# A row gradient on one core: the third load of each group in two transfers, and the first store tied to the first of them

## The chip, the core and the metric

The kernel runs on one core of one Trainium2 chip. The time is device microseconds of one execution. Before the change the median of three runs is 1246.87 us (1246.65 to 1247.15). Next to these stands one profiled execution, whose records are the views shown here; it has a time of its own.

## The reference

```python
def setup_inputs():
    return {"x": np.random.randn(8192, 8192).astype(np.float32)}

def reference(x):
    return np.gradient(x, axis=1)
```

Along each row, an inner element of the result is half the difference of its two neighbours, `(x[j+1] - x[j-1]) / 2`. The two ends of a row are plain differences, `x[1] - x[0]` and `x[8191] - x[8190]`. 268.4 MB are read and as many written.

## The kernel before

The 8192 rows are cut into 32 tiles of 256 rows. Each of the 128 partitions holds two consecutive rows of the input side by side, so a tile is 128 x 16,384 float32, 8.39 MB, and one partition of it is 65,536 contiguous bytes of memory. Three slots in SBUF hold a tile each (`NB = 3`); tile `i` uses slot `i % 3`. A slot has 64 spare columns at its front (`SH = 64`): the input is loaded to columns 64 and up, the result is written in place from column 0, and is stored from there.

For each tile the program issues

- a load (line 52, `load`), on the queue of SyncE (SP), as all transfers;
- on GpSimd (POOL), line 74: the four end differences of the two rows of a partition, into a small tile `ends`; it waits for the load;
- on VectorE (DVE), line 80: one custom instruction over the whole tile that writes half the difference of the neighbours; it waits for line 74;
- line 91: a copy of the four end values to their places, on DVE for 20 tiles and on POOL for 12; it waits for line 80;
- a store (line 56, `store`); it waits for line 91.

The order is written out by hand (`manual_schedule`), so the order of the calls is the order on each engine. `chain` states for an instruction what it needs, and the waits follow from this.

Tiles are worked on in groups of three. The three loads of a group are issued one after another at the end of the group before (lines 103 to 106), each once the store of the tile that had the slot has landed. SP then comes to the group's stores. The first one, of the tile with `i % 3 == 0`, is issued as soon as its tile is finished. The second is held back (`held`, line 100) and carries an extra dependency on line 74 of the third tile (line 94, `at[0]`), that is, on the landing of the third load. The third follows when its tile is finished. All transfers run on the same 16 DMA engines in the order of issue, so reading and writing alternate: three loads, three stores, three loads.

The end differs a little. 32 tiles are ten groups and two tiles. In the last whole group (tiles 27, 28, 29) the loads of tiles 30 and 31 are issued right behind the store of tile 28 (lines 96 to 98), ahead of the store of tile 29; the stores of 30 and 31 end the program.

Of the kernel before, what the change touches and what calls it, by code (L numbers as in the profile page):

```python
# [1 line left out]

# [4 lines left out]


@with_exitstack
def kernel(  # L10
    ctx: ExitStack,
    tc: tile.TileContext,
    x: bass.AP,
    out: bass.AP,
):

    nc = tc.nc
    P = nc.NUM_PARTITIONS
    n, m = x.shape
    R = 2  # L20
    NB = 3
    SH = 64
    W = R * m
    nsets = n // (P * R)
    f32 = x.dtype

    x_sets = x.rearrange("(s p t) m -> s p (t m)", p=P, t=R)
    out_sets = out.rearrange("(s p t) m -> s p (t m)", p=P, t=R)

    pool = ctx.enter_context(tc.tile_pool(name="pool", bufs=1))  # L30
    edge = 256 // 4
    nends = nsets * R * 2
    ends_pad = pool.tile([P, nends + edge // 2], f32, name="ends", tag="ends")
    ends = ends_pad[:, 0:nends].rearrange("p (s t e) -> p s t e", t=R, e=2)
    slots = [pool.tile([P, SH + W], f32, name=f"slot{k}", tag=f"slot{k}") for k in range(NB)]
    loads, stores = [], [None] * nsets
    in_front = {}

    def chain(i, ins, *needed):

        group, engine = f"slot{i % NB}", ins.ins.engine
        keep = [o.ins for o in needed]
        if in_front.get(engine, (None,))[0] == group:
            keep.append(in_front[engine][1])
        tc.declare_no_dep(ins.ins, group=group, keep=keep, reason="implied by the needed step")
        tc.add_to_no_dep_group(group, ins.ins)
        in_front[engine] = group, ins.ins
        return ins

    def load(i):  # L50
        b = slots[i % NB]
        ins = nc.sync.dma_start(out=b[:, SH : SH + W], in_=x_sets[i])  # L52
        loads.append(chain(i, ins, *([stores[i - NB]] if i >= NB else [])))

    def store(i, done, later):
        ins = nc.sync.dma_start(out=out_sets[i], in_=slots[i % NB][:, 0:W])
        stores[i] = chain(i, ins, done)
        if later is not None:
            tc.add_manual_dep(
                ins.ins,  # L60
                later.ins.name,
                mybir.DependencyInfo(mybir.DependencyClass.Sync, mybir.DependencyReason.DATA),
                reason="issued once the next tile has landed",
            )

    held = None
    with tc.manual_schedule():
        for i in range(NB):
            load(i)
        for i in range(nsets):  # L70
            b = slots[i % NB]
            xin = b[:, SH : SH + W].rearrange("p (t m) -> p t m", m=m)

            ins = nc.gpsimd.tensor_sub(  # L74
                out=ends[:, i, :, :],
                in0=xin[:, :, 1 : m : m - 2],
                in1=xin[:, :, 0 : m - 1 : m - 2],
            )
            at = [chain(i, ins, loads[i])]
            ins = nc.vector._custom_dve(  # L80
                dve_ops.TENSOR_TENSOR_REDUCE_SUB_MAX,
                out=b[:, 1 : W - 1],
                in0=b[:, SH + 2 : SH + W],
                in1=b[:, SH : SH + W - 2],
                s0=0.0,
                s1=0.5,
            )
            halved = chain(i, ins, *at)
            res = b[:, 0:W].rearrange("p (t m) -> p t m", m=m)
            placer = nc.gpsimd if i % 5 in (1, 3) and i < nsets - 2 else nc.vector  # L90
            ins = placer.tensor_copy(out=res[:, :, 0 : m : m - 1], in_=ends[:, i, :, :])  # L91
            placed = chain(i, ins, halved)
            if held is not None:
                store(*held, at[0])
                held = None
                if i + 1 + NB > nsets - 1 and i % NB == NB - 1:
                    for k in range(i + 1, nsets):
                        load(k)
            if i % NB == 1 and i + 1 < nsets:
                held = i, placed  # L100
            else:
                store(i, placed, None)
            if i % NB == NB - 1:
                for k in range(i + 1, min(i + 1 + NB, nsets)):
                    if k >= len(loads):
                        load(k)


# [1 line left out]
_INS = ['x']  # L110
_OUTS = [((8192, 8192), 'float32')]


# [23 lines left out]
```

## Time and profile before

| what | value |
|---|---|
| median of three runs | 1246.87 us |
| profiled execution, its own time | 1247.28 us |
| span of its instructions | 1245.4 us |
| moved over the span | 536.88 MB, 431 GB/s |
| DVE busy | 554.6 us (45%) in 52 instructions |
| POOL busy | 8.9 us (1%) in 48 instructions |
| line 80, one instruction | 17.2 us |
| loads, issue to landing (median) | 57.9 us |
| stores, issue to landing (median) | 40.2 us |
| SP, one transfer's issue (median), load and store | 0.339 and 0.343 us |

The page cuts the span into 40 slices; a digit is the busy share of a slice in tenths, and the row GB/s says what the DMA engines moved in it. A group of instructions is shown as line, engine, operation, output<-input, shapes and count, then busy time and mean ns of one, then the idle time of the engine just before them and what ended it. Timeline rows are start, duration (both us), engine, line and operation; a number with x at the end of such a row counts the instructions that are merged in it. SPq is SP's sequencer, which issues the transfers. The transfer records give start, duration and size of every packet on the DMA engines.

### The profile page before, as it was taken

Reading aid. Unit: us, or ns where it says so; the run is one execution under the profiler, and the core shown is the slowest. Engines: PE = TensorE matmul, PEld = TensorE weight load, DVE = VectorE, ACT = ScalarE, POOL = GpSimd, SP = SyncE. Lnnn points to the kernel's source line nnn. Section 1 sums busy time; section 2 is a strip of 40 time slices with the busy share of each in tenths; the row PEclk is TensorE's granted clock in tenths of the full one; section 3 lists DMA queues with packets and bytes.
Section 4 is the critical chain, followed back from the end, with each engine's and each line's share of the span. In section 5 each row is a group of like instructions: output and inputs, shape, how many; then the busy total and the mean of one; then the engine's idle time right before and its main releaser. Section 6 shows DMA issues by size and latency. Waiting matters only on the chain.

```text
span 1245.4 us, 237 instructions
## 1 busy us (share of the span) xinstructions
DVE 554.6 (45%) x52; POOL 8.9 (1%) x48
## 2 busy tenths in 40 slices
DVE  2850483069009702850583079009603840591460
POOL 0000000000000000000000000000000000000000
DMA  9999999999999999999999999999999999999998
GB/s 404 436 432 415 436 438 438 438 438 436 434 427 425 432 438 438 436 425 436 429 432 436 438 438 429 436 432 438 432 429 434 438 432 438 438 429 436 432 432 370
DMA packets 9217, 536.88 MB, mean 431 GB/s; under 512 B 1024, under 2 KB 1024, under 8 KB 1024
## 3 DMA queue, kind: packets, MB, share of 16 engines
q1 hardware_dynamic: 9216, 536.88, 99.7%
q14 instruction: 1, 0.01, 0.0%
HBM read 268.44 MB, written 268.44 MB: 431 GB/s over the span
## 4 chain that ended last, share of the span: by engine, by line
another core or an unknown queue 67%; DVE 18%; DMA 10%; issue 2%; POOL 1%; SPq 0%; POOLq 0%
DVE slot L80 18%; DMA slot<-in_x_dram 6%; DMA out_dram<-slot 3%; POOL ends L74 0%; POOL slot L91 0%; SPq L52 0%; DVE slot L91 0%; POOLq L132 0%
## 5 line engine op out<-in xcount | busy, mean ns | idle before, releaser
L80 DVE CUSTOM_DVE_ANT_0 slot<-slot 128x16382 f32<-128x16382 f32 x32 | 551.2, 17224 | 649.0 <-POOL ends L74 649.0
L74 POOL TENSOR_TENSOR ends<-slot 128x4 f32<-128x4 f32 x32 | 6.4, 200 | 969.9 <-DMA slot<-in_x_dram 969.9
L91 POOL COPY slot<-ends 128x4 f32<-128x4 f32 x12 | 2.3, 192 | 207.9 <-DVE slot L80 207.9
L91 DVE COPY slot<-ends 128x4 f32<-128x4 f32 x20 | 3.4, 172 | 0.7
L121 POOL MEMSET const-bfloat16-1.0<- 128x1 bf16 x1 | 0.1, 102 | 0.0
L121 POOL MEMSET const-uint8-127<- 128x1 uint8 x1 | 0.1, 102 | 0.0
L121 POOL MEMSET const-float32-0.0<- 128x1 f32 x1 | 0.1, 99 | 0.2 <-issue 0.2
L121 POOL MEMSET const-float32-1.0<- 128x1 f32 x1 | 0.1, 99 | 0.0
## 6 DMA issues: line engine op xcount, KB each, us to landing
slot<-in_x_dram SPq DMA_DIRECT2D x32, 57.9
out_dram<-slot SPq DMA_DIRECT2D x32, 40.2
```

The source lines that it names most:

```text
L74: ins = nc.gpsimd.tensor_sub(out=ends[:, i, :, :], in0=xin[:, :, 1 : m : m - 2], in1=xin[:, :, 0 : m - 1 : m - 2],)
L80: ins = nc.vector._custom_dve(dve_ops.TENSOR_TENSOR_REDUCE_SUB_MAX, out=b[:, 1 : W - 1], in0=b[:, SH + 2 : SH + W], in1=b[:, SH : SH + W - 2],
L91: ins = placer.tensor_copy(out=res[:, :, 0 : m : m - 1], in_=ends[:, i, :, :])
L121: nc = _bacc.Bacc("TRN2", target_bir_lowering=False, num_devices=1)
```

## The change

The third load of each group, and the load of the last tile, is issued as two transfers: the first 15,104 columns, then the last 1,280 (`LAST`). Both wait for the same earlier store. `loads[i]` becomes a list of parts, and line 74 of the tile waits for all of them. The group's first store gets an extra dependency on the first part of the group's third load; in the two-tile end, the store of tile 29 gets one on the first part of the load of tile 31. The held second store keeps its dependency on line 74 of the third tile, the third store has none, as before. The instructions on POOL and DVE and their order are the same. SP has 75 transfers in place of 64: 11 loads are split, those of tiles 2, 5, ... 29 and of tile 31, and the order of the stores and the loads among each other stays.

```diff
+    LAST = 1280
@@
     def load(i):
         b = slots[i % NB]
-        ins = nc.sync.dma_start(out=b[:, SH : SH + W], in_=x_sets[i])
-        loads.append(chain(i, ins, *([stores[i - NB]] if i >= NB else [])))
+        freed = [stores[i - NB]] if i >= NB else []
+        cuts = [0, W - LAST, W] if i % NB == NB - 1 or i == nsets - 1 else [0, W]
+        parts = []
+        for lo, hi in zip(cuts, cuts[1:]):
+            ins = nc.sync.dma_start(out=b[:, SH + lo : SH + hi], in_=x_sets[i][:, lo:hi])
+            parts.append(chain(i, ins, *freed))
+        loads.append(parts)
@@
-                reason="issued once the next tile has landed",
+                reason="issued once this load has landed",
@@
-            at = [chain(i, ins, loads[i])]
+            at = [chain(i, ins, *loads[i])]
@@
             if i % NB == 1 and i + 1 < nsets:
                 held = i, placed
             else:
-                store(i, placed, None)
+                turn = loads[-1][0] if i % NB == 0 or i == nsets - NB else None
+                store(i, placed, turn if len(loads[-1]) > 1 else None)
```

## The prediction

> **What bounds the kernel now.** I read four views in this order: the page's slices of the span, the groups of instructions, the timeline around two ends of a group, and the transfer records in short stretches. The page comes first:
>
> ```profile
> DVE  2850483069009702850583079009603840591460
> DMA  9999999999999999999999999999999999999998
> GB/s 404 436 432 415 436 438 438 438 438 436 434 427 425 432 438 438 436 425 436 429 432 436 438 438 429 436 432 438 432 429 434 438 432 438 438 429 436 432 432 370
> ...
> L80 DVE CUSTOM_DVE_ANT_0 slot<-slot 128x16382 f32<-128x16382 f32 x32 | 551.2, 17224 | 649.0 <-POOL ends L74 649.0
> L74 POOL TENSOR_TENSOR ends<-slot 128x4 f32<-128x4 f32 x32 | 6.4, 200 | 969.9 <-DMA slot<-in_x_dram 969.9
> ```
>
> The 16 DMA engines are full in every slice; VectorE works 45% and always ends up waiting for a load. So only what the DMA engines lose can be won. Best slices move 438 GB/s, many 425 to 432. Where is the difference? In the timeline a POOL instruction of line 74 begins about 0.4 us after its load's last packet, so these rows are the loads' landings. Two ends of a group:
>
> ```profile
> 42.27 17.22 DVE L80 CUSTOM_DVE_ANT_0 slot<-slot 128x16382 f32<-128x16382 f32 x1 [1.85 <-POOL ends L74]
> ...
> 62.74 0.20 POOL L74 TENSOR_TENSOR ends<-slot 128x4 f32<-128x4 f32 x1 [2.99 <-DMA slot<-in_x_dram]
> 62.97 17.80 SPq L56 DMA_DIRECT2D out_dram<-slot  x2
> ```
>
> ```profile
> 390.28 40.12 SPq L56 DMA_DIRECT2D out_dram<-slot  x3
> 391.97 0.20 POOL L74 TENSOR_TENSOR ends<-slot 128x4 f32<-128x4 f32 x1 [19.17 <-DMA slot<-in_x_dram]
> ...
> 412.33 0.20 POOL L74 TENSOR_TENSOR ends<-slot 128x4 f32<-128x4 f32 x1 [20.16 <-DMA slot<-in_x_dram]
> ```
>
> The third load of the group landed 62.74 - 42.04 = 20.70 us after the second in the one (42.04 is the POOL row just ahead of the first line shown), 412.33 - 391.97 = 20.36 us in the other; other loads that follow a load come 19.1 to 19.3 us after it. The loss sits where a group's loads give way to its stores. A short stretch of the transfer records shows it (40 slices of 0.25 us; a packet is booked where it starts):
>
> ```profile
> GB/s 0 0 2359 1311 524 0 0 0 0 0 0 262 2884 524 524 0 0 0 0 0 0 0 0 0 0 0 262 2884 786 262 0 0 0 0 0 0 786 2621 524 262
> ```
>
> This is 55 to 65 us. Each DMA engine carries one row of 65,536 B at a time, 2.418 us each, so bursts of 16 starts should stand 2.4 us apart. They stand at 55.6, 58.1, then only at 61.8: the last packet of the third load took 1.2 to 1.4 us too long on all 16 engines, just ahead of the first store. I chained all packet records engine by engine. Almost every lengthened packet is the last one of a third load (a few are the first of the next loads); stores stay at 2.42 but for two or three. The amounts per engine are 1.2 to 1.4 us at the first switch, 0.3 to 1.05 at the fourth (412 us), 0 to 0.7 at the others. Over the run the engine that ends last collected 5.05 us of this, the four luckiest about 1.85 each. So 1.85 us falls on all engines together and 3.2 us is the lag of one engine behind the others: first landings and last landings of a transfer stand 0.6 us apart at the beginning and 3.5 us at the end.
>
> A check from the landings alone: the first loads of the groups come at 22.76 and, nine groups later, 1070.70, so a group takes 116.44 us, the quietest 115.87; 9 x 0.57 = 5.1 us. That is the whole prize.
>
> **The change, part by part.**
>
> *The wait.* The group's first store (line 56) was issued at 390.28, some 20 us before the engines could reach it; at 40.45 and 157.83 likewise. Now it waits for the first part of the third load, so SP holds it until then. Behind it on SP stand the group's second store, which already waited for the third load (issued at 62.97, 0.23 us after the landing), the third store, and the next loads, which wait for stores; none could go earlier than this point, and the second store is needed only 19.3 us after the first has begun. So nobody else becomes late. VectorE and POOL wait for both parts, which is the old landing. At the tail, the store of tile 29 was issued at 1148.34 with two loads ahead of it; it moves to about 1185, and the next one (1185.03 before) follows at once. That makes 11 switches, ten groups and the tail.
>
> *What it removes.* While the third load's last full packets run, no store stands behind them, and engines that are ahead can't begin to write while others still read; every engine starts its stores from the same issue, so the lag is cut back at each switch instead of adding up. The trace of before never shows a switch without a queued store, so the price has two ends: nothing (the stall belongs to the change of direction itself) and 5.05 us (all of it). The 3.2 us of lag I take whole. Of the 1.85 us on all engines I take 1.3, because there no engine was writing yet when it occurred, so the queued store is the nearest thing to blame, but not the only one. Removed: 4.5 us.
>
> *What it adds in packets.* Each split gives each engine 8 packets of 60,416 B and 8 of 5,120 B for 8 of 65,536 B, and one more 4 B semaphore packet. Bytes are the same. 11 x 8 = 88 extra packets on each engine. The nearest row is the 4 B packet, recorded at 9 ns: 88 x 9 ns = 0.8 us. Low end 0, since 8 packets of 2.418 us fill the 19.3 us of a transfer with no visible remainder. High end: the only packets that started on an empty engine, the first of the run, took 0.68 us longer (median engine); once per tail, 7.5 us. I take 0.8, as the tail stands in a full queue. The added issue instruction costs SP 0.34 us (median of line 52) at a time when its transfer lands some 58 us later: nothing.
>
> *What it adds in idle engines.* This decides. After the last packet of the first part on the slowest engine, at T, the next issue on SP starts at T+0.37 (81.69 to 82.07, 197.79 to 198.15 between a store's last packet and the load that waited for it). From issue to first packet there is one place where the queue was empty, the start:
>
> ```profile
> 0.74 1.33 SPq L52 DMA_DIRECT2D slot<-in_x_dram  x3
> ```
>
> ```profile
> GB/s 0 0 0 0 0 0 0 3670 262 262 0 0 0 0 0 0 0 0 0 2359 1311 524 0 0 0 0 0 0 262 3146 262 524 0 0 0 0 0 0 1049 2359
> ```
>
> (0 to 10 us.) Fourteen engines start at 1.75 to 1.99, the last two at 2.17 and 2.34: 1.0 to 1.6 us after the issue. So stores are there at T+1.38, at worst T+1.97. The tail that covers this is 1280/16384 of 19.31 us = 1.51 us, 1.58 with its packet cost. Fourteen engines are covered to within 0.05 us, two may not be. The first issue of a run took SP 0.38 us against 0.34 later, so a warm one is rather quicker. I take 0.03 us for a switch, 11 x 0.03 = 0.3 us. The ends are 0 (an idle time can't be negative) and 0.46 of gap plus 0.68 for a packet on an empty engine, 1.14 us a switch or 12.5 us.
>
> The Trainium skill speaks against this ("DMA: Bandwidth & Descriptors", section "Anatomy of one DMA — SWDGE (gpsimd) path"): a DMA has about 2.0 us of fixed cost, mostly the receipt for its last write. That figure is for transfers issued by GpSimd, these come from SP, and the trace shows 1.38 us for last packet, issue and first packet together. With 2.0 in its place each switch would lie idle 0.42 us, estimated from that page's figure, and the sum would come out at +0.9 us.
>
> *Sum.* -4.5 + 0.8 + 0.3 = -3.4 us. The profiled execution took 1247.28 us (span 1245.4 and 1.9 around it): 1243.9. It is 0.41 us above the median of the three runs, 1246.87, so the forecast is **1243.5 us**.
>
> **Rivals.**
>
> *The queue runs dry at the switch (slower).* The first part's landing, the issue and the generation of 128 descriptors don't fit under 1.51 us, and the engines drain; each then also starts its store packet without the next one overlapped. For it: the two engines at 1.97 us, and the 0.68 us of the run's first packets. Against it: fourteen engines at 1.38 to 1.62. A switch costs c; with all 5.05 us removed the sum is 11c + 0.8 - 5.05, which is 0 at c = 0.39 and reaches +2.5 us at c = 0.61. With c = 0.85, between there and the 1.14 of the end, it is +5.1: **1252.0 us**; at 1.14 it is +8.3, 1255.1.
>
> *Gap and gain cancel.* c is 0.2 to 0.4, or the long last packets remain because changing direction costs them whoever is queued. For it: at the first switch all engines stalled alike, without any lag. Against it: at 876 us no engine stalled at all, so the change of direction alone has no fixed price. With c = 0.3 and 4.5 removed: 3.3 + 0.8 - 4.5 = -0.4, **1246.5 us**; with nothing removed and no gap, +0.8, 1247.7.
>
> *The wait never binds.* Then only the 0.8 us of packets is left, 1247.7 us. The store was ready about 21 us before that landing in the groups I looked at, so I give this no chance of its own.
>
> **How the numbers follow.** A change under 0.2% (2.5 us) can't be told from none here. The forecast case, own range 1242.0 to 1244.4, has 0.45; cancelling, 1244.4 to 1249.4, has 0.27; the dry queue, above that, 0.28. These are also the chances of faster, same and slower. The range runs from 1241.5 (all 5.05 removed at almost no cost, and the 0.3 us by which single runs differ) to 1252.5, just past the middle of the dry case; it leaves out the upper half of that, 0.14, and little below.
>
> **What would show it.** Right: the third load's first part lands about 1.5 us before the second, the store's issue stands 0.4 us behind it, its packets follow the tail with under 0.1 us between, bursts of starts stand within 0.7 us to the end of the run, and groups take 115.9 to 116.2 us. Dry queue: a hole in the DMA starts at each switch, the stretch from tail to first store packet above 0.4 us, and groups near 117. Wrong in the gain: last packets still lengthened at 60 and 410 us. The prediction fails if issue to first packet is much above 1.1 us on a warm SP, or if 5,120 B packets take well over 0.2 us each.

## The result, and the profile after

The changed kernel takes 1255.14 us (median of six runs, 1254.83 to 1255.73), the kernel before 1247.09 us beside it: ratio 1.0065, 95% interval 1.0052 to 1.0078. It is slower by 8 us, where 3.4 us of gain were forecast, and lies above the range. The profiled execution has a span of 1253.8 us against 1245.4.

The page of the changed kernel; line 86 is the old line 80 on VectorE, line 80 the old line 74 on POOL:

```profile
DMA  9999999999999999999999999999999999999999
GB/s 401 435 435 433 433 406 435 435 427 443 435 408 444 420 435 435 435 435 410 432 429 435 435 424 445 435 402 446 424 424 427 420 435 435 432 438 424 424 422 401
...
L86 DVE CUSTOM_DVE_ANT_0 slot<-slot 128x16382 f32<-128x16382 f32 x32 | 551.2, 17224 | 656.9 <-POOL ends L80 656.9
L80 POOL TENSOR_TENSOR ends<-slot 128x4 f32<-128x4 f32 x32 | 6.4, 200 | 977.7 <-DMA slot<-in_x_dram 977.7
```

VectorE's work is the same to the tenth; it waits 7.9 us longer. The DMA engines still count as full in every slice, so the loss is not a hole that this row can show: packets took longer. The landings tell how evenly it is spread. The first loads of consecutive groups now land 116.86 to 117.67 us apart, all nine of them; before, three of nine stood at 115.87 to 115.97.

The turn from loads to stores in the second group, in the changed kernel's timeline:

```profile
177.68 19.65 SPq L62 DMA_DIRECT2D out_dram<-slot  x3
179.30 0.20 POOL L80 TENSOR_TENSOR ends<-slot 128x4 f32<-128x4 f32 x1 [19.50 <-DMA slot<-in_x_dram]
179.54 17.22 DVE L86 CUSTOM_DVE_ANT_0 slot<-slot 128x16382 f32<-128x16382 f32 x1 [2.27 <-POOL ends L80]
```

The store is issued at 177.68, 0.36 us behind the last packet of the first part (177.32 in the packet records) and 1.6 us ahead of the landing of the second. The transfer records from 172 to 182 us of the same run, in slices of 0.25 us:

```profile
GB/s 1933 725 0 483 0 0 0 0 725 2175 483 0 483 0 0 0 0 102 307 369 369 471 369 369 164 61 3711 524 0 0 0 0 0 0 0 1311 2621 262 0 0
```

The low figures from the 18th slice on are the short packets of the tail; the two high ones behind them are all 16 engines starting the store at 178.5 to 178.9. Between the tail and the store an engine lies idle 0.40 us on average in this turn, and 0.16 over the 11 turns (0.01 to 0.51). The tail runs through in 1.55 us on every engine and the store is there 1.2 us behind the slowest first part, so the slowest engine is covered; an engine that ended its first part over 0.34 us earlier is not, and here the first parts ended up to 0.93 us apart. This turn works nearly as forecast.

The other turn, from the third store to the next loads, does not. From 112 to 122 us, the changed kernel:

```profile
GB/s 786 0 0 0 0 0 0 0 1049 2621 524 0 0 0 0 0 0 0 3146 1049 0 0 0 0 0 0 0 0 0 0 1049 1311 1573 262 0 0 0 0 0 0
```

and the same stretch of the kernel before:

```profile
GB/s 0 524 2621 786 262 0 0 0 0 0 0 1835 1835 524 0 0 0 0 0 0 0 2621 1049 524 0 0 0 0 0 0 524 2622 786 262 0 0 0 0 0 0
```

Before, the bursts of starts stand 2.4 us apart straight through the turn at 119.7. After, the burst at 116.6 is followed by one at 119.5 to 120.3: the last packet of the third store takes 0.43 to 1.09 us too long on every engine. In this document such an excess is called a stall: the time of a packet above its usual 2.418 us. In the kernel before this happened at none of ten such turns; now it happens at all ten, with a mean between 0.61 and 0.71 us at each.

Taken as means over the 16 engines, from the packet records:

| loss, us in the whole run | before | after |
|---|---|---|
| last packets of loads, ahead of the first stores | 2.6 | 0.0 |
| idle ahead of the first stores | 0 | 1.8 |
| first packets of the first stores | 0.0 | 0.4 |
| last packets of third stores, ahead of loads | 0.0 | 6.7 |
| first packets of those loads | 0.1 | 1.0 |
| first parts of the third loads | - | 1.7 |
| tails of 5,120 B packets beyond the time for their bytes | - | 0.4 |

Before, the engine that ended last had 5.05 us in the first row because the engines had drifted apart; after, all are within 0.3 us at most turns to the loads, so the mean is the end. The losses after add up to 12.0; less 5.05 that is 7 of the 8.4 us between the spans. Another 0.6 lies behind the last packet, where the program ends (1.2 us before, 1.8 after); the rest is not assigned. No run was made for the 1.7 us in the first parts, which fall on packets in the middle of these transfers; with a longer second part, 2048 columns, they are 0.2.

### The profile page after: what moved, and what is told of

It reads as the page before. It is cut to its first block, busy times and chain, and to the rows that moved or that the text cites. A ratio compares the mean times of both kernels' runs of the same rounds, so it can differ in the third digit from the quotient of the medians.

```text
span 1253.8 us, 266 instructions
## 1 busy us (share of the span) xinstructions
DVE 554.6 (44%) x52; POOL 8.9 (1%) x48
## 4 chain that ended last, share of the span: by engine, by line
another core or an unknown queue 68%; DVE 18%; DMA 9%; POOL 1%; issue 0%; SPq 0%; POOLq 0%
DVE slot L86 18%; DMA slot<-in_x_dram 6%; DMA out_dram<-slot 3%; POOL ends L80 0%; POOL slot L97 0%; SPq L57 0%; POOLq L139 0%; POOLq L80 0%; DVE slot L97 0%
```

## Experiments

Three theories were put up for the stall ahead of the loads. A: it depends on whether the first store was standing in the queue when the engines came to it. B: the wait brings 16 engines in step and they stall one another. C: the split load with its short packets does it. "Stall ahead of the loads" is below always the excess of the last packets of a third store, a mean over the engines, taken in the one profiled execution of a run. Every ratio is to the kernel before, timed beside that run; the times themselves were taken on several chips.

**The wait taken out, the split kept.**

```diff
-                turn = loads[-1][0] if i % NB == 0 or i == nsets - NB else None
-                store(i, placed, turn if len(loads[-1]) > 1 else None)
+                store(i, placed, None)
```

> The third load is split as in the change, the first store's extra wait is taken out. In the changed kernel the time is lost in a place the prediction did not name: the last packet of each third store, just ahead of the next loads, takes 0.4 to 1.1 us too long on all 16 engines (0.69 on average), which it never does in the kernel before. Theory A (empty start): a first store that begins on engines with nothing queued costs them the read-ahead that hides the first reads of the next loads. Theory B (in step): the wait brings the engines in step, and 16 engines that turn from writing to reading together stall each other. Theory C (split): the short packets or the added transfer do it. A and B: 1247 to 1248 us, no long packet ahead of the loads, the long one at the first turn from loads to stores (about 1.3 us) back. C: 1252 us or more, with the stall ahead of the loads.

1248.70 us, 1.0012 of the kernel before (1.0003 to 1.0022), a little above the 1247 to 1248 of A and B. No stall ahead of the loads at any of ten turns, and the one ahead of the first store is back: 1.20 us at the first turn, 0.32, 0.26, 0.34 at the next. The records from 112 to 122 us, the turn at 119.7 without a gap:

```profile
GB/s 0 262 2097 1311 262 262 0 0 0 0 0 1049 1835 786 524 0 0 0 0 0 0 1573 2097 0 524 0 0 0 0 0 262 2097 1311 262 262 0 0 0 0 0
```

The wait is the cause; the split alone costs some 1.4 us.

**The wait in every second group.**

```diff
-                store(i, placed, turn if len(loads[-1]) > 1 else None)
+                store(i, placed, turn if len(loads[-1]) > 1 and i // NB % 2 == 0 else None)
```

> As the changed kernel, but the first store waits for the first part of the third load only in every second group (tiles 0, 6, 12, 18, 24 and 30). Theory A (empty start): the last packet of the third store is long (0.4 to 1.1 us) in the groups that wait and at 2.42 us in those that don't, although the engines are in step within 0.5 us in both; about 1251 us. Theory B (in step): it is long in both kinds, since a group without the wait starts with engines that the group before has put in step; 1253 to 1256 us.

1255.79 us: not the 1251 of theory A but in the range of B, yet the stall ahead of the loads is as A has it, 0.65 to 0.72 us in the five groups that wait and 0.00 in the five that don't. Two turns of this run, from 347 and from 464 us on:

```profile
GB/s 0 0 0 0 0 0 0 3932 262 0 0 0 0 0 0 0 2097 2097 0 0 0 0 0 0 0 0 0 0 1573 1311 1311 0 0 0 0 0 0 0 262 2884
```

```profile
GB/s 1573 1311 262 0 0 0 0 0 262 1311 1835 786 0 0 0 0 0 0 262 1835 1835 262 0 0 0 0 0 262 786 1573 1311 262 0 0 0 0 0 262 1311 1573
```

In the first (a group that waits) 3.0 us lie between the burst at 351.1 and the loads at 354.1; in the second (no wait) every distance is 2.4. Where the time went instead: the groups without the wait pay 0.43 to 1.17 us ahead of their first store. So the stall does not vanish in either kind of group, it changes its place. B isn't excluded here, since the engines of the groups without the wait were 0.6 to 1.7 us apart.

**Eight engines taken out of step.** An extra transfer of 8 partitions x 8192 columns to a spare tensor follows the first store:

```diff
+                if i % NB == 0 and i + NB < nsets:
+                    ins = nc.sync.dma_start(
+                        out=spare[:, i * SKEW : (i + 1) * SKEW], in_=b[0:8, 0:SKEW]
+                    )
+                    extra[i] = chain(i, ins, placed)
```

> As the changed kernel, with an additional transfer of 8 partitions x 8192 columns behind the first store of each group into a spare tensor in memory, which occupies eight of the engines for about 1.2 us and so takes them out of step before the turn to the loads. It adds about 10 x 1.2 = 12 us by itself. Theory A (empty start): the last packets of the third stores stay 0.4 to 1.1 us too long on all engines; about 1267 us. Theory B (in step): with eight engines 1.2 us behind the other eight they are under 0.3 us; about 1261 us.

1311.15 us in a single execution. The extra transfer held its eight engines 4.6 to 5.3 us, not 1.2. At the first turn to the loads, about a dozen packets near the end of the third store took up to 0.8 us too long and about twenty of the load behind it up to 1.3 us: neither all engines at their last packet, as A had it, nor almost nothing, as B. The engines were two packets apart, much more than planned, and the run doesn't tell the theories apart.

**The tail longer.** The constant `LAST` is 4096, 2560, 2048 and 1536 in place of 1280, nothing else, so that the store's packets are ready ever earlier.

> As the changed kernel, but the second part of the third load has 4096 columns, 4.8 us of work in place of 1.5, so that the store's packets stand in the queue some 3.4 us before the engines reach them. Theory A (empty start): the engines never run empty, the stall ahead of the loads is gone (0 to 0.1 us), the one ahead of the first store returns in part; 1245 to 1248.5 us. Theory B (in step): the engines stay within 0.6 us of one another at least in the first groups, so the stall ahead of the loads stays there, 0.4 to 1.0 us; 1249 to 1254 us. Theory C (split): still a stall at each group, 1252 us or more.

> The changed kernel with a tail of 1536 columns (1.8 us) in place of 1280 (1.5 us); one of a series on how far ahead of the engines the first store's packets must be. By the runs so far a store's first packet can start 0.85 us after its issue, and the issue follows 0.4 us behind the first part, so the packets are ready about 0.5 us before the engines get to them. Theory A (empty start): between the two ends, the stall ahead of the next loads 0 to 0.7 us, all engines alike; 1246 to 1254 us. Theory B (in step): the engines still meet the turn within 0.4 us of each other, stall 0.6 to 0.7 us; 1253 to 1256 us.

> The same with 2048 columns (2.4 us): the packets are ready about 1.1 us ahead. Theory A (empty start): the stall ahead of the loads under 0.2 us, the one of 1.0 to 1.3 us at the first turn to the stores back; 1245 to 1249 us. Theory B (in step): 0.6 to 0.7 us in each group where the engines are within 0.4 us, so at least in the first ones; 1250 to 1255 us.

> The same with 2560 columns (3.0 us): ready about 1.7 us ahead. Theory A (empty start): as with 4096 columns, no stall ahead of the loads; 1245 to 1248.5 us. Theory B (in step): as with 2048 columns, 1249 to 1254 us.

| columns in the tail | time, us | ratio to before (95%) | stall ahead of the loads, us | ahead of the first stores, us |
|---|---|---|---|---|
| 1280 (the change) | 1255.14 | 1.0065 (1.0052 to 1.0078) | 0.61 to 0.71 | 0.00 |
| 1536 | 1251.92 | 1.0047 (1.0033 to 1.0062) | 0.45 to 0.70 | 0.00 to 0.01 |
| 2048 | 1248.34 | 1.0019 (1.0009 to 1.0028) | 0.02 to 0.66 | 0.00 to 0.01 |
| 2560 | 1250.31 | 1.0023 (1.0011 to 1.0034) | 0.01 to 0.66 | 0.00 to 0.23 |
| 4096 | 1247.93 | 1.0005 (0.9996 to 1.0014) | 0.00 to 0.06 | 0.00 to 1.02 |

The times with 1536, 2048 and 4096 columns lie in the ranges of A, the one with 2560 only in that of B; with 2048 the stall that A expected back at the first turn to the stores stayed away. The ten executions with 2560 columns ran from 1244.8 to 1251.6 us, further apart than in any other run of the series.

The run with 2048 columns decides against B. In four of its groups (turns at 469, 585, 701 and 817 us) the engines came to the turn within 0.28 to 0.46 us of one another, about as in step as in the changed kernel (0.16 to 0.36), and stalled 0.02 to 0.09 us. With 1536 columns they came within 0.35 to 0.57 us and stalled 0.45 to 0.70. The records with 2048 columns from 580 to 590 us:

```profile
GB/s 2359 1835 0 0 0 0 0 0 0 262 3408 524 0 0 0 0 0 0 0 786 3408 0 0 0 0 0 0 0 0 2097 2097 0 0 0 0 0 0 0 0 2884
```

All distances are 2.4 us, the turn at 585.0 among them. In these groups the store's first packet started 1.58 to 1.76 us after its issue, so it had waited in the queue 0.73 to 0.91 us. In the same run, groups where it started after 0.85 to 1.2 us stalled 0.39 to 0.66. The first group doesn't fit: its store started after 1.55 us and it stalled 0.57, but there some engines still lay idle, for up to 0.19 us, until their own first packet came. With 2560 columns theory A expected no stall and was wrong in most groups: the engines drifted some 2 us apart there, the issue waits for the slowest, and for the fast ones the store came too late again (0.84 us from issue to first packet in three groups).

**No split, the store waits for the whole third load.**

```diff
-        cuts = [0, W - LAST, W] if i % NB == NB - 1 or i == nsets - 1 else [0, W]
+        cuts = [0, W]
@@
-                store(i, placed, turn if len(loads[-1]) > 1 else None)
+                store(i, placed, turn)
```

> No split: the group's first store waits for the whole third load, so each engine lies idle until the store is there. Both theories: the stall ahead of the loads as in the changed kernel, 0.6 to 0.7 us, since the engines are both empty and in step. The idle time is 0.4 us to the issue and 0.85 us to the first packet, 1.25 us on the last engine, 11 times; with the 2.5 us or so of the short packets gone and no cover, 1263 to 1268 us. It prices what the split is worth.

1268.48 us, 1.0180 (1.0159 to 1.0200), just above the expected 1263 to 1268. A stall of 0.65 to 0.68 us ahead of the loads, without any split. Its timeline and its records from 174 to 184 us:

```profile
179.87 18.04 SPq L62 DMA_DIRECT2D out_dram<-slot  x3
179.89 0.20 POOL L80 TENSOR_TENSOR ends<-slot 128x4 f32<-128x4 f32 x1 [19.11 <-DMA slot<-in_x_dram]
```

```profile
GB/s 1049 2097 1049 0 0 0 0 0 0 0 1835 1835 524 0 0 0 0 0 0 0 0 0 0 0 0 0 1835 2359 0 0 0 0 0 0 0 0 2359 1835 0 0
```

The last load packets start at 176.5 to 177.2 and take 2.4 us; the store starts at 180.7. The hole is 1.48 to 1.86 us a turn on average over the engines, where 1.25 was expected for the last engine alone: that one lies idle about 1.4 us, and the others wait for it. Longer emptiness costs its own time but no more stall: 0.67 against 0.67.

**The store issued by VectorE's progress, no split.** VectorE's instruction on the second tile ends shortly before the third load does. The first store is held until that instruction, or, with `CUT` columns split off as a second instruction, until its first piece.

```diff
+            steps = [1, W - 1]
+            if first is not None and CUT:
+                steps = [1, W - 1 - CUT, W - 1]
+            for lo, hi in zip(steps, steps[1:]):
...
+                halved = chain(i, ins, *at)
+                if first is not None:
+                    store(*first, halved)
+                    first = None
...
+            elif i % NB == 0 and i < nsets - NB or i == nsets - NB:
+                first = i, placed
```

> The kernel before, with no split load; the group's first store is issued when VectorE's instruction of the second tile (line 80) has ended, which by the timeline before lies 1.4 us ahead of the last packet of the third load on the slowest engine. With 0.85 us from issue to first packet the store is ready about 0.55 us ahead of that engine, less ahead of the faster ones. Theory A (how far ahead the store is ready decides): by the series of tails (0 us ahead 0.7 us of stall, 0.3 us 0.5, 0.6 us 0.1, 0.9 us 0.02) a stall of 0.1 to 0.4 us ahead of the loads, none ahead of the stores, no short packets; 1242 to 1246 us. If the short packets of the split mattered (theory C), nothing of the loss would be left: 1241 to 1242 us.

> The same, with VectorE's instruction of the second tile cut in two, 256 columns in the second, and the store issued after the first: 0.3 us earlier, so ready about 0.85 us ahead. Theory A: under 0.1 us of stall at either turn, groups of 115.9 to 116.2 us, 1241 to 1243.5 us. If the stall ahead of the loads came from the split or from engines in step, it would be there at 0.6 to 0.7 us, 1248 us or more.

> The same with 512 columns: ready about 1.1 us ahead. Theory A: no stall ahead of the loads, some of the stall ahead of the first stores back (0.1 to 0.5 us at the first turns, less later); 1242 to 1246 us.

> The store issued by VectorE's instruction as before, with 768 columns in the second piece: another 0.27 us earlier, so ready about 1.0 us ahead of the engines where they are in step (0.75 us with 512 columns). By the runs so far the stall ahead of the loads is about 0.7 us less the time by which the store was ready ahead of the engine that reaches it first. Theory A: 0 to 0.1 us ahead of the loads in most groups, a little ahead of the stores; 1243 to 1246.5 us, the first version that could beat the kernel before. If the stall doesn't follow that time, 1247 us or more.

| `CUT` | time, us | ratio to before (95%) | stall ahead of the loads, us |
|---|---|---|---|
| 0 | 1249.86 | 1.0022 (1.0013 to 1.0032) | 0.54 to 0.71 |
| 256 | 1248.31 | 1.0014 (1.0004 to 1.0024) | 0.26 to 0.64 |
| 512 | 1246.91 | 0.9999 (0.9989 to 1.0008) | 0.06 to 0.57 |
| 768 | 1246.90 | 1.0000 (0.9991 to 1.0009) | 0.10 to 0.62 |

With `CUT` 0 the timeline has the store at VectorE's end, 1.8 us ahead of the landing:

```profile
393.37 17.22 DVE L86 CUSTOM_DVE_ANT_0 slot<-slot 128x16382 f32<-128x16382 f32 x1 [1.90 <-POOL ends L76]
410.63 2.40 SPq L57 DMA_DIRECT2D out_dram<-slot  x2
...
412.45 0.20 POOL L76 TENSOR_TENSOR ends<-slot 128x4 f32<-128x4 f32 x1 [19.11 <-DMA slot<-in_x_dram]
```

and the records from 463 to 473 us still show the long last packets (3.0 us from the burst at 467.1 to the loads at 470.1):

```profile
GB/s 0 0 0 0 0 0 0 2884 1311 0 0 0 0 0 0 0 1573 2097 524 0 0 0 0 0 0 0 0 0 1311 1835 1049 0 0 0 0 0 0 0 1835 2097
```

Together with the plain wait above, that is a second stall with no split load in the kernel, against C. All four times came out above what was expected, by 3.9, 4.8, 0.9 and 0.4 us beyond the upper ends. I had put the store 0.55 us ahead of the engines with `CUT` 0; the records show 0.00 to 0.2 us ahead of the first one. None of these versions beats the kernel before: 512 and 768 equal it.

**All of them together.** For each turn to the stores I took how long the store had stood ready (time from issue to its first packet on any engine, less the 0.85 us that this takes when nothing is in front), and set it against the stall at the next turn to the loads. From the changed kernel and nine of the runs above (not the ones with the extra transfer, the wait taken out, and 2560 columns; the ten turns of the last follow the same line: 0.56 to 0.66 us of stall where the store was not ahead, 0.20 to 0.35 at 0.4 to 0.7 us, 0.05 at 0.9):

| store ready ahead, us | turns | stall ahead of the loads, mean (range) | stall ahead of the store, mean |
|---|---|---|---|
| under 0.02 | 32 | 0.67 (0.57 to 0.72) | 0.00 |
| 0.02 to 0.25 | 22 | 0.55 (0.27 to 0.64) | 0.00 |
| 0.25 to 0.4 | 8 | 0.40 (0.34 to 0.48) | 0.00 |
| 0.4 to 0.6 | 10 | 0.27 (0.22 to 0.32) | 0.00 |
| 0.6 to 0.8 | 10 | 0.18 (0.06 to 0.57) | 0.00 |
| 0.8 to 1.1 | 3 | 0.06 (0.02 to 0.13) | 0.00 |
| 1.0 to 4.0 (4096 columns) | 10 | 0.01 (0.00 to 0.06) | 0.19 |
| about 20 (groups without the wait) | 5 | 0.00 | 0.81 |

The stall is about 0.7 us less the time for which the store was ready. It holds for the split, for VectorE's clock and for the plain wait alike. Between 0.7 and 1 us both turns are nearly free, but for the first groups of two runs (2048 columns and `CUT` 512: 0.57 and 0.50 us of stall), in which engines still lay idle ahead of the store; with a store queued long before, the cost shows ahead of the store. The first packets of the run, which also started on empty engines, took 0.7 us too long as well. The records show the dependence; why a store that was ready early should spare the loads behind it, and whether the read-ahead named in theory A is the reason, they don't show.

## Why the prediction was wrong

- *What bounds the kernel*: right. Only DMA time moved the end, and the long packets at the turns were the loss.
- *The wait and the queue behind it*: right. Nothing behind the store on SP became late; the store of tile 29 moved to 1192.9 us, against about 1185 in the forecast, as all before it was later.
- *What it adds in idle engines*: nearly right. The issue follows 0.36 us behind the first part, as put at 0.37; the first packet comes 0.85 us after the issue where 1.0 to 1.6 was read off the cold start. 1.8 us of idle time in the run against 0.3. The forecast took the time from the slowest engine and the cover as if all 16 ended their first part with it; engines that were ahead ran out of tail first.
- The about 2.0 us of fixed cost that the Trainium skill ("DMA: Bandwidth & Descriptors", section "Anatomy of one DMA — SWDGE (gpsimd) path") gives for transfers issued by GpSimd is not what these transfers, issued by SP, show: 0.36 and 0.85 us, 1.21 together.
- *What it adds in packets*: too high for the tails, 0.4 us measured against 0.8: a tail takes 1.55 us. The 4 B packet that set the price is no addition of 9 ns in these records: the data packet behind it starts before it has ended. The 1.7 us in the first parts were not forecast.
- *What it removes*: the step that failed. "Removed: 4.5 us" was met where it was looked for: the stall ahead of the first stores went to 0.00 and the engines stayed within 0.3 us of one another at most turns to the loads. All of the 5.05 us is gone, a little more than the 4.5 in the sum. But the sum held that nothing takes its place, and no term stood for the turn from stores to loads, which had cost 0.00 before. There the changed kernel loses 6.7 us, and 1.0 us in the load packets behind it. I had left that turn's zero standing without a reason; it was a result of the store standing in the queue early.
- *The dry queue*: its time, 1255.1 us at 1.14 us a switch, is close to the result, but not for its reason. It has the loss as idle time and slow packets where the store begins; measured there are 0.16 us a turn and store packets within 0.05 us of their usual length. That the number is close is luck. A tail of 1.5 us was nearly enough against idleness, and 0.9 us too short against the stall that comes 58 us later: 2048 columns, 2.4 us, made both turns nearly free in four groups.
- *Gap and gain cancel* is what 4096 columns and VectorE's clock with `CUT` 512 and 768 came to in time, though with a stall at the other turn in place of the gap.

## What to carry to other kernels

A queue that hardly runs empty is not enough. Where a kernel on full DMA queues turns from loads to stores, measure both turns, because the price of a late issue can show at the next one; in this kernel both were nearly free where the store stood ready 0.7 to 1 us before the engines reached it. A stall that is absent from a profile is a fact of that schedule, not of the operation; before taking its zero into the sum of a changed schedule, ask what keeps it at zero. Against a schedule with transfers queued some 20 us ahead, issue at the last moment had at most 5 us of 1247 to win here, and none of the ten variants that were timed won any.

## What the runs showed that I had not expected

- From an issue on SP to the first packet on an idle engine it is 0.85 us, to within 0.01 us at most of 22 turns (the changed kernel and the plain wait). At the start of the run, before, it was 1.0 us.
- A transfer of 8 partitions x 32,768 B from SBUF runs on eight engines, but each packet takes 4.6 to 5.3 us, 8 x 32,768 B in about 5 us, 52 GB/s in all. A 128-partition transfer moves 65,536 B per engine in 2.42 us. So half the bytes took twice as long on the same engine; no run here shows why.
- Issue by the landing of the slowest engine keeps the 16 engines within about 0.3 us of one another at most turns to the loads; with queued stores the first and the last landing of one transfer are 3.6 us apart by the middle of the run.
